# Ordering a few small TensorE products behind named dense products in a two-layer hybrid decoder trunk

## The chip, the core and the metric

The kernel runs on one core of one Trainium2 chip. The metric is the device time of one execution in microseconds (us), as the median of several runs. The core's engines are named as the profile names them: PE is TensorE, PEld its loads of weights, DVE is VectorE, ACT is ScalarE, POOL is GpSimd, and SP is the engine whose queue issues the DMA transfers.

## The reference, cut to what matters

Two layers are computed for 512 tokens of width 1024, in float32. Each layer norms its input, projects it, feeds three branches in parallel, merges them by gates, and ends with a wide MLP.

```python
xn = rmsnorm(x, norm1_g)
proj = xn @ w_in
y_ssd = ssd_mixer(...)      # chunked state-space scan, 2 groups of 8 heads, chunks of 128 tokens
y_mla = mla_mixer(...)      # latent attention, 8 heads
y_gdn = gdn_mixer(...)      # gated delta rule, 8 value heads, chunks of 64 tokens
mixed = g_ssd * (y_ssd @ w_ssd_out) + g_mla * (y_mla @ w_mla_out) + g_gdn * (y_gdn @ w_gdn_out)
h = x + mixed @ w_out
x = h + jnp.square(relu(rmsnorm(h, norm2_g) @ w_up)) @ w_down
```

Within a chunk the state-space branch multiplies its tokens by a decayed matrix of products of B and C (`y_diag`), adds what the state of the earlier chunks gives, multiplies by a gate and norms each group. The delta rule needs, for each chunk, the matrix of products of its keys, weighted by decays, and the inverse of that matrix plus the identity.

## The kernel before, in words

**Dense products.** Every large product is made by `dense_F` (or by its transposed twin). Operands are split into a high and a low part in a 32-bit format that PE takes in one pass, and `mm3` (lines 182 to 184) makes three PE instructions of each 128x128 by 128x512 product: high by high, high by low, low by high. A product with 256 output columns and 1024 inputs is 48 such instructions. Its weights come in four pairs of 128-row steps: each pair holds 12 instructions (column tile 0 with both steps, then column tile 1), and is split by a cast on ACT (L154) and a subtraction on DVE (L155). The split tiles rotate through four buffers, so that a cast waits until PE has finished with the pair four before. Raw weights come by DMA on SP's queue (L161).

**Small products.** Transpositions, chunk products and state updates are plain float32 instructions. They write to three rotating PSUM banks (`sm_bank`), with a fourth one apart (`y_bank`); dense products have four of their own.

**Order of the work.** The kernel is written in Tile: the text gives each instruction a place, and a scheduler of the compiler builds the queue of each engine from a model of the durations. An instruction earlier in the text goes first if its inputs are ready in that model; if not, later work is put ahead of it. `tc.high_priority()` lifts the splits (L154, L155) and the convolutions (L700 to L704). On the chip each engine takes its queue in order, and an instruction whose input is late holds what is queued behind it.

**The order around the change.** Per layer, the text reads: first state-space group, the decays of the delta rule (`gdn_decays`), the first half of the attention's output (`out_proj` with parts 0 and 1), second state-space group, the other half (parts 2 and 3), key products of the delta rule, and the state-space branch's output product. Each part of `out_proj` is a gate product (48 dense instructions on the normed input, `xh` and `xl` in the profile), then an output product (48 on the branch's result, `yh` and `yl`). So the scan of a state-space group, which has many small steps, is laid between the dense instructions of the gate and output product that follow it in the text.

- `ssd_group`, t = 0 to 3: products of B and C (L756), masked on DVE (L758), times the decays (L760), which ACT makes from a broadcast row (L467, L468, loaded at L465); then **the decay products** (L765, 8 products, 16 PE records), added on DVE (L767); for t > 0 the part of the earlier state (L774 to L776); the state update (L779, L781, L784 to L787); the gate (L790), squares (L792 to L794) and their sums (L795).
- After the four blocks: **the norm factors** (`rsq`: DVE L258, then a power on POOL, L259), **their transposition** on PE (L799), a copy on ACT (L801), a write to DRAM and a broadcast read (L802, L804 on SP), and the normed result (L808) with its split.
- `key_tiles` makes 256 key columns by a dense product, then convolution taps on ACT and DVE (L700, L704) and an activation that ends in DVE L263 and gives the tiles `ft`.
- `gdn_matrix(u, kT)`: **the key products** of four token tiles (L846), their masked copies and diagonal sums on DVE (L850, L851), then the power on POOL (L853, L855, L856) and the matrices (L861, L869). Unit 0 is called after the first `key_tiles`, so its products run among the dense instructions of the second `key_tiles`; unit 1 is called by `between` within the output product of the state-space branch. `gdn_blocks` and `gdn_inverse` use both units' matrices later (first PE step L925, fed by the copies at L919).

Of the kernel before, what the change touches and what calls it, by code (L numbers as in the profile page):

```python
# [20 lines left out]
P = 128  # L21
S = 512
T = S // P
D = 1024
# [31 lines left out]
def hybrid_kernel(ctx, tc, a, out, depth=2, taps=None):  # L56
# [89 lines left out]
        act.activation(cosT, nn, AF.Sin)  # L146


    def split_half(raw, hold=None, first=True):

        n = raw.shape[1]
        hi, lo = hold or (mk(wp, [P, n], F32R, "whi"), mk(wp, [P, n], F32R, "wlo"))
        with tc.high_priority() if first else nullcontext():
            act.copy(hi, raw)  # L154
            dve.tensor_tensor(lo, raw, f32(hi), ALU.subtract)  # L155
        return hi, lo
# [8 lines left out]
    def weights(w2d, c0, n, K, hold=None, raw0=None):  # L165

        kt = min(1024 // n, K // P)  # L170
        step = 512 // n
        for k0 in range(0, K // P, kt):
            given = raw0 is not None and k0 == 0
            raw = raw0 if given else weights_raw(w2d, c0, n, k0, kt)
            for q in range(0, kt, step):
                hi, lo = split_half(raw[:, q * n : (q + step) * n], hold and hold[k0 + q], not given)
                v = lambda x: x.rearrange("p (k n) -> p k n", n=n)
                yield k0 + q, v(hi), v(lo)

    def mm3(o, ah, al, bh, bl, start, stop, more=False):  # L180

        pe.matmul(o, ah, bh, start=start, stop=False, skip_group_check=more)  # L182
        pe.matmul(o, ah, bl, start=False, stop=False, skip_group_check=more)  # L183
        pe.matmul(o, al, bh, start=False, stop=stop, skip_group_check=more)  # L184

    def dense_F(gen, cols, K, xh, xl, mid=None, banks=None, after=None):

        pss = banks or [acc_bank() for _ in cols]
        last = K // P - 1
        if mid:
            gen = list(gen)
            for i, hf in enumerate(HALVES):
                for ps, c in zip(pss, cols):
                    for k0, wh, wl in gen:
                        for k in range(wh.shape[1]):  # L200
                            kk = k0 + k
                            mm3(ps[:, hf], wh[:, k, c], wl[:, k, c], xh[kk][:, hf], xl[kk][:, hf], kk == 0, kk == last)
                if i == 0:
                    mid()
            return pss
        for k0, wh, wl in gen:
            for ps, c in zip(pss, cols):
                for k in range(wh.shape[1]):
                    a_, b_ = wh[:, k, c], wl[:, k, c]
                    mm3(ps[: a_.shape[1], :], a_, b_, xh[k0 + k], xl[k0 + k], k0 + k == 0, k0 + k == last)  # L210
            if after:
                after()
        return pss
# [145 lines left out]
    xh, xl = hilo_tags(lp, "x")  # L359
# [4 lines left out]
    for ly in range(depth):  # L364
# [107 lines left out]
        def out_proj(w2d, br, yh, yl, pl, part=range(4), after=None, make=None, gate_banks=lambda: None):  # L472
            for dp in part:
                tg = []
                for j, ps in enumerate(dense_F(weights(w_in, O_GATE + br * D + dp * 256, 256, D), tiles(256), D, xh, xl, None, gate_banks(), after)):
                    t_ = make(dp, j) if make else mk(pl, [P, S], F32, "cva", 2)
                    act.activation(t_, ps, AF.Tanh, scale=0.5)
                    tg.append(t_)
                for j, ps in enumerate(dense_F(weights(w2d, dp * 256, 256, D), tiles(256), D, yh, yl, after=after)):
                    d = 2 * dp + j  # L480
                    if mixed[d] is None:
                        mixed[d] = mk(lp, [P, S], F32, "mix", 8)
                        dve.scalar_tensor_tensor(mixed[d], tg[j], 1.0, ps, ALU.add, ALU.mult)
                    else:
                        with tc.high_priority() if make else nullcontext():
                            dve.scalar_tensor_tensor(tg[j], tg[j], 1.0, ps, ALU.add, ALU.mult)
                            dve.tensor_tensor(mixed[d], mixed[d], tg[j], ALU.add)
# [227 lines left out]
        def ssd_group(g, yh, yl):  # L715
# [34 lines left out]
            for t in range(T):  # L750
                tok = slice(t * P, (t + 1) * P)
                e2 = [mk(br, [P, 4, P], F32, "eE", 4) for _ in range(2)]
                for q in range(2):
                    seg_exp(e2[q], t, h0 + 4 * q)
                ps = sm_bank()
                pe.matmul(ps[:, :P], bt[:, tok], ctl[:, tok], start=True, stop=True)  # L756
                cb = mk(br, [P, P], F32, "gk", 2)
                dve.scalar_tensor_tensor(cb, ps[:, :P], 0.25, incl, ALU.mult, ALU.mult)  # L758
                for e in e2:
                    dve.tensor_tensor(e, e, bc_mid(cb, 4), ALU.mult)  # L760
                py = sm_bank()
                for c in range(4):
                    for i in range(2):
                        h = 2 * c + i
                        pe.matmul(py[64 * i : 64 * i + 64, c * P : (c + 1) * P], xd[:, t, h * 64 : (h + 1) * 64], e2[h // 4][:, h % 4, :], start=True, stop=True)  # L765
                y = xf[:, :, tok]
                dve.tensor_tensor(y, y, c4(py), ALU.add)  # L767
                if t > 0:
                    eb = mk(br, [P, 4, P], F32, f"wk{t % 2}")
                    for i in range(2):  # L770
                        sync.dma_start(eb[64 * i : 64 * i + 64], d_p.rearrange("t (n l) -> t n l", l=P)[t, h0 + i : h0 + 8 : 2].partition_broadcast(64))
                    po = sm_bank()
                    for c in range(4):
                        pe.matmul(po[:, c * P : (c + 1) * P], st[:, c * P : (c + 1) * P], ctl[:, tok], start=True, stop=True)  # L774
                    dve.tensor_tensor(eb, c4(po), eb, ALU.mult)
                    dve.tensor_tensor(y, y, eb, ALU.add)  # L776
                if t < T - 1:
# [12 lines left out]
                dve.tensor_tensor(zt, zt, y, ALU.mult)  # L790
                sq = mk(br, [P, 4, P], F32, "wk2")
                act.activation(sq, zt, AF.Square)  # L792
                dve.tensor_tensor(sq[:, 0:2], sq[:, 0:2], sq[:, 2:4], ALU.add)
                dve.tensor_tensor(sq[:, 0], sq[:, 0], sq[:, 1], ALU.add)  # L794
                pe.matmul(pss[:, t : t + 1], sq[:, 0], ones[:, 0:1], start=True, stop=True)  # L795
            rs = mk(sp, [P, T], F32, "srs")
            rsq(rs, pss[:, :T], 1.0 / 512, EPS)
            ps = sm_bank()
            pe.transpose(ps[:T, :P], rs, ident)  # L799
            rsT = mk(br, [T, P], F32, "gk", 2)  # L800
            act.copy(rsT, ps[:T, :P])  # L801
            sync.dma_start(d_r[g].rearrange("(t p) -> t p", p=P), rsT)  # L802
# [19 lines left out]
        def key_tiles(c0, after=None):  # L822

            res = [mk(br, [P, S], F32, "ft", 6) for _ in range(2)]
            for i, ps in enumerate(dense_F(weights(w_in, O_GQ + c0 * P, 256, D), tiles(256), D, xh, xl, after=after)):
                gconv_silu(ps, c0 + i, res[i])
            return res

# [8 lines left out]
        def gdn_matrix(u, kT):  # L837
# [4 lines left out]
            for t in range(T):  # L842
                tok = slice(t * P, (t + 1) * P)
                pg = sm_bank()
                for i in range(2):
                    pe.matmul(pg[:, i * P : (i + 1) * P], kT[i][:, tok], kT[i][:, tok], start=True, stop=True)  # L846
                gk = mk(br, [P, 2, P], F32, f"wk{t}")
                for i in range(2):

                    dve.scalar_tensor_tensor(gk[:, i], hv(pg)[:, i], 1.0, ident, ALU.mult, ALU.mult, accum_out=ssq[:, i, t : t + 1])  # L850
                dve.tensor_tensor(gk, hv(pg)[:, 0:2], bc_mid(nstrict, 2), ALU.mult)  # L851
                gks.append(gk)
# [568 lines left out]
```

## Time and profile before

| | us |
|---|---|
| median of 3 runs | 2303.87 (2301.91 to 2304.52) |
| the profiled execution | 2301.75 |
| span of its first to last instruction | 2300.0 |
| PE busy | 2269.1 |
| DVE busy | 1645.3 |
| ACT busy | 1202.2 |
| POOL busy | 59.3 |

The profile is of one execution. A timeline row is: start in us from the span's start, duration, engine, line, operation, out<-in, shapes, count, and in brackets the idle time of the engine before it with what ended it. PE records overlap, since an instruction enters the array while the one before it is still in it: the distance from start to start tells what one costs, not the duration. In the view of waits a row is: who waited, for whom, us in total, times, longest. An idle time there counts from the modelled end of the instruction before. PE's granted clock was 0.999 of full speed over the span.

### The profile page before, as it was taken

To read this page: it belongs to the slowest core of one execution; us is meant where nothing else is said; L and a number is where in the kernel's file an instruction comes from. 1 tells how busy PE (TensorE), PEld (TensorE's weight loads), DVE (VectorE), ACT (ScalarE), POOL (GpSimd) and SP (SyncE) were. 2 spreads that over 40 slices of the span, in tenths; PEclk is the share of its full clock that TensorE was granted. 3 is DMA by queue.
4 is the path that set the end of the run, shared out by engine and by line. 5 is a ranking of instruction groups with operands and counts; after the bars stand their busy time and mean duration, and the time that the engine had idled before them with its cause. 6 is when DMAs were issued, how large, how long until landed. Compare 5 with 4: busy or idle time off the path is not lost.

```text
span 2300.0 us, 32300 instructions
## 1 busy us (share of the span) xinstructions
PE 2269.1 (99%) x11822; PEld 1864.8 (81%) x11822; DVE 1645.3 (72%) x3258; ACT 1202.2 (52%) x2508; POOL 59.3 (3%) x75
## 2 busy tenths in 40 slices
PE   9999999999999999999999999999999999999998
PEld 8788787888887888888888877878888877888886
DVE  7777566876667778767867775668657667778668
ACT  6766644334443465554657666443334435645545
POOL 0000000000000000000000000000000000000000
PEclk9999999999999999999999999999999999999999
DMA  4223634452224243233132236344422241433231
GB/s 144 81 74 101 193 101 119 126 141 75 87 69 165 65 147 108 86 109 111 53 99 78 79 108 195 95 113 141 126 77 83 65 165 56 160 106 101 92 110 46
DMA packets 220176, 244.23 MB, mean 106 GB/s; under 512 B 34272, under 2 KB 172528, under 8 KB 220016
## 3 DMA queue, kind: packets, MB, share of 16 engines
q1 hardware_dynamic: 220016, 242.16, 34.7%
q8 instruction: 93, 1.52, 0.3%
q14 instruction: 67, 0.55, 0.1%
HBM read 225.66 MB, written 11.74 MB: 103 GB/s over the span
## 4 chain that ended last, share of the span: by engine, by line
PE 89%; DVE 4%; ACT 2%; POOL 1%; issue 1%; DMA 0%; DVEq 0%; POOLq 0%; ACTq 0%; SPq 0%
PE acc L182 23%; PE acc L183 22%; PE acc L184 22%; PE sm L182 3%; PE sm L183 3%; PE sm L184 3%; DVE wlo L155 1%; PE sm L765 1%; PE sm L663 1%; ACT whi L154 1%; PE sm L1049 1%; POOL gms L259 1%; PE sm L774 1%; PE yt L679 1%; PE sm L643 1%
## 5 line engine op out<-in xcount | busy, mean ns | idle before, releaser
L155 DVE TENSOR_TENSOR wlo<-wraw,whi 128x512 fp32r<-128x512 f32 (+1 forms) x536 | 365.0, 685 | 344.8 <-ACT whi L154 338.2
L154 ACT CAST whi<-wraw 128x512 fp32r<-128x512 f32 (+1 forms) x536 | 329.7, 618 | 535.5 <-PE acc L183 365.3
L184 PE MATMUL acc<-xh,wlo 128*128 128x512 f32 (+1 forms) x1344 | 522.4, 389 | 0.0
L182 PE MATMUL acc<-xh,whi 128*128 128x512 f32 (+1 forms) x1344 | 522.2, 389 | 0.0
L183 PE MATMUL acc<-xl,whi 128*128 128x512 f32 (+1 forms) x1344 | 521.4, 388 | 0.0
L182 PEld LDWEIGHTS acc<-xh,whi 128*128 128x128 f32 x1344 | 252.7, 188 | 48.0 <-ACT xh L254 0.4
L183 PEld LDWEIGHTS acc<-xl,whi 128*128 128x128 f32 x1344 | 252.9, 188 | 47.7 <-DVE xl L255 0.7
L184 PEld LDWEIGHTS acc<-xh,wlo 128*128 128x128 f32 x1344 | 252.8, 188 | 47.7
L154 ACT CAST whi<-wr 128x512 fp32r<-128x512 f32 x168 | 104.3, 621 | 107.6 <-PE acc L183 47.5
L183 PE MATMUL acc<-yl,whi 128*128 128x512 f32 x384 | 151.4, 394 | 0.0
L182 PE MATMUL acc<-yh,whi 128*128 128x512 f32 x384 | 150.8, 396 | 0.0
L184 PE MATMUL acc<-yh,wlo 128*128 128x512 f32 x384 | 149.9, 390 | 0.0
L155 DVE TENSOR_TENSOR wlo<-wr,whi 128x512 fp32r<-128x512 f32 x168 | 113.2, 686 | 35.3 <-ACT whi L154 34.4
L704 DVE SCALAR_TENSOR_TENSOR ckl<-acc,pc,ckl 128x511 f32<-128x511 f32 (+2 forms) x168 | 120.3, 743 | 18.0 <-ACT ckl L700 10.8
L182 PEld LDWEIGHTS acc<-yh,whi 128*128 128x128 f32 x384 | 71.6, 188 | 16.0 <-ACT yh L254 1.7
L184 PEld LDWEIGHTS acc<-yh,wlo 128*128 128x128 f32 x384 | 72.2, 188 | 14.5
L183 PEld LDWEIGHTS acc<-yl,whi 128*128 128x128 f32 x384 | 72.2, 188 | 13.7
L183 PE MATMUL acc<-wlo,xh 128*128 128x512 f32 (+1 forms) x208 | 79.9, 384 | 0.0
L184 PE MATMUL acc<-whi,xl 128*128 128x512 f32 (+1 forms) x208 | 79.5, 384 | 0.0
L182 PE MATMUL acc<-whi,xh 128*128 128x512 f32 (+1 forms) x208 | 79.5, 384 | 0.0
L1161 DVE TENSOR_TENSOR h<-h,acc 128x512 f32<-128x512 f32 x120 | 76.9, 679 | 0.0
L467 ACT ACTIVATE eE<-eE,cum 128x128 f32<-128x128 f32 x192 | 63.2, 390 | 25.3 <-DMA eE<-d_c 22.2
(462 smaller groups left out, 4553.7 us busy)
## 6 DMA issues: line engine op xcount, KB each, us to landing
wraw<-in_w_in_dram SPq DMA_DIRECT2D x144, 512.0 KB, 3.6
wraw<-in_w_up_dram SPq DMA_DIRECT2D x64, 512.0 KB, 3.6
wr<-in_w_down_dram SPq DMA_DIRECT2D x32, 1024.0 KB, 5.3
eE<-d_c SPq DMA_DIRECT2D x48, 256.0 KB, 4.0
wraw<-in_w_mla_out_dram SPq DMA_DIRECT2D x16, 512.0 KB, 3.5
eE<-d_e SPq DMA_DIRECT2D x32, 256.0 KB, 2.8
wraw<-in_w_ssd_out_dram SPq DMA_DIRECT2D x16, 512.0 KB, 3.4
wraw<-in_w_gdn_out_dram SPq DMA_DIRECT2D x16, 512.0 KB, 3.4
```

What stands on the lines that cost most here:

```text
L154: act.copy(hi, raw)
L155: dve.tensor_tensor(lo, raw, f32(hi), ALU.subtract)
L182: pe.matmul(o, ah, bh, start=start, stop=False, skip_group_check=more)
L183: pe.matmul(o, ah, bl, start=False, stop=False, skip_group_check=more)
L184: pe.matmul(o, al, bh, start=False, stop=stop, skip_group_check=more)
L259: pool.tensor_tensor(o, o, (exp if exp is not None else nhalf)[:, : o.shape[1]], ALU.pow)
L467: act.activation(o[:, i], o[:, i], AF.Relu, scale=-1.0, bias=cum[:, t, h0 + i : h0 + i + 1])
L643: pe.matmul(o, qps[j][:, tok], kps[:, :n], start=False, stop=False)
L663: pe.transpose(ps[:, n : n + P], pn[t][:, kb * P : (kb + 1) * P], ident)
L679: pe.matmul(o, v_h, th[:, c : c + w], start=kb == 0, stop=False)
L704: dve.scalar_tensor_tensor(acc[:, d:], ps[:, : S - d], taps_[3 - d], acc[:, d:], ALU.mult, ALU.add)
L1161: dve.tensor_tensor(hs_, hs_, ps[t], op)
```

## The change

`behind(key, ins)` records that PE's instruction `ins` is to come after the dense product with that key; `place(key, ins)`, called by `dense_F` at the third instruction of each product, gives the key its instruction. The link (`NoSync`) is one for the scheduler's order alone: both instructions are PE's, and no semaphore is asked for. A key is (tag, row step k, column tile j). `dense_F` gets a tag from its callers: layer, branch, part and "g" (gate) or "y" (output) in `out_proj`, layer, "k" and the first key column tile in `key_tiles`.

```diff
+    def after_product(i, o):
+        tc.add_manual_dep(i, o.name, order_only, reason="behind a product")
+    def behind(key, ins):
+        if key in seen_at:
+            after_product(ins.ins, seen_at[key])
+        else:
+            awaiting.setdefault(key, []).append(ins.ins)
+    def place(key, ins):
+        seen_at[key] = ins.ins
+        for i in awaiting.pop(key, ()):
+            after_product(i, ins.ins)
...
-            for ps, c in zip(pss, cols):
+            for j, (ps, c) in enumerate(zip(pss, cols)):
                 for k in range(wh.shape[1]):
                     a_, b_ = wh[:, k, c], wl[:, k, c]
-                    mm3(ps[: a_.shape[1], :], a_, b_, xh[k0 + k], xl[k0 + k], k0 + k == 0, k0 + k == last)
+                    end = mm3(ps[: a_.shape[1], :], a_, b_, xh[k0 + k], xl[k0 + k], k0 + k == 0, k0 + k == last)
+                    place((tag, k0 + k, j), end)
...
-                        pe.matmul(py[64 * i : 64 * i + 64, c * P : (c + 1) * P], xd[:, t, h * 64 : (h + 1) * 64], e2[h // 4][:, h % 4, :], start=True, stop=True)
+                        x = pe.matmul(py[64 * i : 64 * i + 64, c * P : (c + 1) * P], xd[:, t, h * 64 : (h + 1) * 64], e2[h // 4][:, h % 4, :], start=True, stop=True)
+                        if t == 0:
+                            behind(((ly, 1, 2 * g, "g"), 2, 0), x)
...
-            pe.transpose(ps[:T, :P], rs, ident)
+            behind(((ly, 1, 2 * g, "y"), 6, 0), pe.transpose(ps[:T, :P], rs, ident))
...
-                    pe.matmul(pg[:, i * P : (i + 1) * P], kT[i][:, tok], kT[i][:, tok], start=True, stop=True)
+                    x = pe.matmul(pg[:, i * P : (i + 1) * P], kT[i][:, tok], kT[i][:, tok], start=True, stop=True)
+                    if u == 0:
+                        behind(((ly, "k", 6), *((4, 1) if t < 3 else (6, 0))), x)
```

So in each layer, for both state-space groups, the decay products of t = 0 come behind step 2, column tile 0 of the gate product of the part that follows the group, and the transposition of the norm factors behind step 6, column tile 0 of that part's output product. In each layer unit 0's key products come behind step 4, column tile 1 (tiles 0 to 2) and step 6, column tile 0 (tile 3) of the second key product. Nothing is computed otherwise.

More of the change, by code (lines that the diff above doesn't have):

```diff
@@ L146, in rope_tables @@
         act.activation(cosT, nn, AF.Sin)
+    seen_at, awaiting = {}, {}
+    order_only = mybir.DependencyInfo(mybir.DependencyClass.NoSync, mybir.DependencyReason.DATA)
+    def after_product(i, o):
[9 more added lines that the diff above has]
+            after_product(i, ins.ins)
     def split_half(raw, hold=None, first=True):
@@ L183, in mm3, with dense_F @@
         pe.matmul(o, ah, bl, start=False, stop=False, skip_group_check=more)
-        pe.matmul(o, al, bh, start=False, stop=stop, skip_group_check=more)
-    def dense_F(gen, cols, K, xh, xl, mid=None, banks=None, after=None):
+        return pe.matmul(o, al, bh, start=False, stop=stop, skip_group_check=more)
+    def dense_F(gen, cols, K, xh, xl, mid=None, banks=None, after=None, tag=None):
         pss = banks or [acc_bank() for _ in cols]
@@ L474, in out_proj @@
                 tg = []
-                for j, ps in enumerate(dense_F(weights(w_in, O_GATE + br * D + dp * 256, 256, D), tiles(256), D, xh, xl, None, gate_banks(), after)):
+                for j, ps in enumerate(dense_F(weights(w_in, O_GATE + br * D + dp * 256, 256, D), tiles(256), D, xh, xl, None, gate_banks(), after, (ly, br, dp, "g"))):
                     t_ = make(dp, j) if make else mk(pl, [P, S], F32, "cva", 2)
@@ L478, in out_proj @@
                     tg.append(t_)
-                for j, ps in enumerate(dense_F(weights(w2d, dp * 256, 256, D), tiles(256), D, yh, yl, after=after)):
+                for j, ps in enumerate(dense_F(weights(w2d, dp * 256, 256, D), tiles(256), D, yh, yl, after=after, tag=(ly, br, dp, "y"))):
                     d = 2 * dp + j
@@ L824, in key_tiles @@
             res = [mk(br, [P, S], F32, "ft", 6) for _ in range(2)]
-            for i, ps in enumerate(dense_F(weights(w_in, O_GQ + c0 * P, 256, D), tiles(256), D, xh, xl, after=after)):
+            for i, ps in enumerate(dense_F(weights(w_in, O_GQ + c0 * P, 256, D), tiles(256), D, xh, xl, after=after, tag=(ly, "k", c0))):
                 gconv_silu(ps, c0 + i, res[i])
```

## The prediction

> **What bounds the kernel now.** I read the page first (busy time, then the shares of the chain that ended last), next the view of waits for TensorE alone, and only then the timeline of the places that the change names.
>
> ```profile
> span 2300.0 us, 32300 instructions
> PE 2269.1 (99%) x11822; PEld 1864.8 (81%) x11822; DVE 1645.3 (72%) x3258; ACT 1202.2 (52%) x2508; POOL 59.3 (3%) x75
> ...
> PE 89%; DVE 4%; ACT 2%; POOL 1%; issue 1%; DMA 0%; DVEq 0%; POOLq 0%; ACTq 0%; SPq 0%
> ```
>
> The profiled execution took 2301.75 us: a span of 2300.0 and 1.75 around it. TensorE (PE) is busy for 99% of the span and holds 89% of the chain. So time goes only where PE's stream of products has a hole in it. The holes that these edits can reach are four rows of the waits; columns: total us, times, longest us.
>
> ```profile
> PE sm L799 <- POOL srs L259: 2.3, 4, 0.6
> PE sm L846 <- DVE ft L263: 1.7, 2, 0.8
> ...
> PE sm L765 <- ACT whi L154: 0.7, 3, 0.3
> PE sm L765 <- DVE eE L760: 0.5, 1, 0.5
> ```
>
> The reader is to see how small this is: 5.2 us in all. An idle time counts only from the modelled end of the product before it, so each hole is somewhat deeper. The timeline gives the measure (layer 0, first state-space group).
>
> ```profile
> 228.36 0.48 PE L182 MATMUL acc<-xh,whi 128*128 128x512 f32 x1
> ...
> 230.76 0.39 PE L183 MATMUL acc<-xl,whi 128*128 128x512 f32 x1
> 231.08 1.09 PE L765 MATMUL sm<-eE,tok 128*64 128x128 f32 x16
> ...
> 244.52 0.66 PE L765 MATMUL sm<-eE,tok 128*64 128x128 f32 x8 [0.20 <-ACT whi L154]
> ...
> 249.92 0.39 PE L182 MATMUL acc<-yh,whi 128*128 128x512 f32 x1
> ...
> 260.77 0.40 PE L184 MATMUL acc<-yh,wlo 128*128 128x512 f32 x1
> 261.70 0.27 PE L799 MATMUL sm<-ct,srs 128*4 128x128 f32 x1 [0.54 <-POOL srs L259]
> 261.73 0.48 PE L182 MATMUL acc<-yh,whi 128*128 128x512 f32 x1
> 262.04 0.39 PE L183 MATMUL acc<-yl,whi 128*128 128x512 f32 x1
> ...
> 265.24 0.39 PE L182 MATMUL acc<-xh,whi 128*128 128x512 f32 x1
> ...
> 268.64 0.39 PE L182 MATMUL acc<-xh,whi 128*128 128x512 f32 x1
> ```
>
> A dense product starts every 0.227 us when nothing is between ((268.64 - 265.24) / 15 starts), though its record lasts 0.39; a hole therefore costs 0.39 - 0.227 = 0.16 us more than the waits show. The one after a small product takes 0.31 (261.73 to 262.04): a switch costs 0.09. Entering L765 takes 0.32 (230.76 to 231.08), the same 0.09. One 256-wide dense product is 48 such instructions, so the gate product begins at 228.36: L765 stands behind its 11th instruction (rows 228.36 to 230.76 are 11), and the transposition L799 behind the 33rd instruction of the product that begins at 249.92 (249.92 to 260.77 are 33).
>
> **The change part by part.** It adds no instruction and, on paper, no semaphore: only the order in PE's queue changes. All keys are counted in dense instructions: ("g", 2, 0) is number 15 of a gate product, ("y", 6, 0) number 39 of an output product, (4, 1) and (6, 0) numbers 33 and 39 of the key product.
>
> *Transposition (4 times, L799).* It moves from behind 33 to behind 39: six dense products, 6 x 0.227 = 1.36 us later. Today the 15 dense products queued behind it stand still while the factor's power on POOL ends.
>
> ```profile
> 260.64 1.01 POOL L259 TENSOR_TENSOR srs<-srs,nhalf 128x4 f32<-128x4 f32 x1 [196.34 <-DVE srs L258]
> ```
>
> The power ends at 261.65 and PE goes on at 261.70. The hole is 260.77 to 261.70 less 0.227 = 0.70 us; over the four, 2.3 + 4 x 0.16 = 2.9 us. With six products in front and everything else as it was, PE would arrive at 260.77 + 7 x 0.227 = 262.36, after the power: gain 2.9, the upper bound. If the whole chain of the group shifts by the four products of the next edit (0.91 us), the power ends at 262.56 and 0.25 us of each hole stay: gain 4 x 0.45 = 1.8 to 1.9, the lower bound. I take 2.4, the middle. What is issued later with it:
>
> ```profile
> 262.29 0.32 SPq L802 DMA_DIRECT2D d_r<-gk  x1
> ...
> 268.16 0.43 SPq L161 DMA_DIRECT2D wraw<-in_w_mla_out_dram  x1
> ```
> ```profile
> L808 DVE SCALAR_TENSOR_TENSOR yl<-tok,pc,ft x14: 743/744/752, 394.6 to 1545.3; 128x512 f32<-128x512 f32 x14
> ```
>
> ACT's copy L801 and the 2 KB write L802 move by up to 1.36 us; behind L802 in SP's queue stand decay transfers and, 5.9 us later, a weight load. The factors are first used for normed tiles near 390 us, over 100 us later for this group, so nothing waits for the lateness itself. POOL's order is untouched. If SP's cover were gone, the price would be at most the 1.36 us.
>
> *First block's products (4 times, L765 of t = 0).* They move from behind 11 to behind 15: 0.91 us. The entry of 0.09 has no real hole in it today, so nothing is won at this place. What follows in the group (state product, next block) hangs on the same three small banks, so I expect the group to move as one body, 0.91 us. A gain can come only from how the body then meets the weight splits. The hole in front of 244.52 shows it:
>
> ```profile
> 240.43 0.70 ACT L467 ACTIVATE eE<-eE,cum 128x128 f32<-128x128 f32 x2 [1.35 <-DMA eE<-d_c]
> 241.03 0.61 ACT L154 CAST whi<-wraw 128x512 fp32r<-128x512 f32 x1
> 241.67 0.69 DVE L155 TENSOR_TENSOR wlo<-wraw,whi 128x512 fp32r<-128x512 f32 x1 [0.57 <-ACT whi L154]
> ```
>
> ACT waits for a decay tile, its cast comes late, and DVE's L155 stands in the middle of the group's chain: 0.57 idle + 0.69 = about 1.2 us, overlap taken off. That cast waits for the release of the second pair of weights (number 23); with four more products ahead of the block, the release comes before the next block's products and the split can fall into an earlier idle time. Bounds: all L765 holes, 0.7 + 0.5 + 4 x 0.16 = 1.8 less the four entries of about 0.09, so 1.5 us won; one more split in each group's chain, 4 x 1.2 = 4.8 lost. I take 0.5 won, near nothing, because the row to which it is nearest, the entry of 0.09, is no hole.
>
> *Key products (twice, L846 of unit 0).*
>
> ```profile
> 413.66 0.39 PE L182 MATMUL acc<-xh,whi 128*128 128x512 f32 x1
> ...
> 419.56 1.50 PE L846 MATMUL sm<-ft 128*128 128x128 f32 x12
> ...
> 422.04 0.60 PE L846 MATMUL sm<-ft 128*128 128x128 f32 x4
> ...
> 432.25 0.39 PE L184 MATMUL acc<-xh,wlo 128*128 128x512 f32 x1
> 433.48 0.94 PE L846 MATMUL sm<-ft 128*128 128x128 f32 x6 [0.84 <-DVE ft L263]
> ```
>
> From 413.66 there are 26 dense instructions to unit 0's first three tiles and 5 more to its last. They move to 33 and 39: 1.6 and 1.8 us later. Neither has a hole today; the whole 1.7 us of the waits' row is unit 1's, which the diff does not order. But the chain of waits leads from that hole back through unit 0:
>
> ```profile
> 425.11 1.65 POOL gork L855
> ...
> 426.79 0.17 DVE gork L856
> ...
> 427.41 0.66 DVE ckl L704
> ```
> ```profile
> 425.19 0.69 ACT L700 ACTIVATE ckl<-acc,pc 128x512 f32<-128x512 f32 x1 [0.97 <-PE acc L184]
> ```
>
> The convolution of unit 1's key could start on DVE at 425.19 + 0.69 = 425.88, but its first tap runs at 427.41: in DVE's queue it stands behind L856, which waits for POOL's power. With unit 0 some 1.6 us later the power would start near 426.7, after the taps are ready; a plan that fills DVE by readiness then puts the taps first, 1.5 us earlier, and POOL's power beside them. Unit 1's hole is 433.48 - 432.25 - 0.227 = 1.0 us, 1.7 + 2 x 0.16 = 2.0 for both layers; 1.5 covers it, and I take 1.9. Bounds: 2.2 won, with a saved switch of 0.09 in each layer; on the other side unit 0's lateness goes on to the block inverses.
>
> ```profile
> 501.31 0.62 ACT L919 COPY tok<-wk 32x512 f32<-32x512 f32 x1 [3.31 <-DMA wk<-d_x]
> ```
> ```profile
> 502.94 1.20 PE L925 MATMUL sm<-wk,tok 32*32 32x32 f32 x64
> ```
>
> The inverses' blocks are in at 501.31, 1.6 us before PE asks for them. PE, 1.0 us faster, would leave 0.6; if all of 1.8 us arrived there, PE would wait 1.2 us, 2.4 in both layers. DVE's recovered idle time (1.5) speaks against it.
>
> One rule speaks against this step. First the rows: POOL's power for four columns takes 1.01 at 260.64, but 1.52 when it starts just behind a DVE split with two inputs in SBUF; a split that starts inside a power is not held (0.69), nor is that power (1.64).
>
> ```profile
> 626.83 1.52 POOL L259 TENSOR_TENSOR gms<-gms,nhalf 128x4 f32<-128x4 f32 x1 [17.58 <-DVE gms L258]
> ```
> ```profile
> 626.79 0.69 DVE L155 TENSOR_TENSOR wlo<-wraw,whi 128x512 fp32r<-128x512 f32 x1
> ...
> 443.68 0.69 DVE L155 TENSOR_TENSOR wlo<-wraw,whi 128x512 fp32r<-128x512 f32 x1 [0.46 <-ACT whi L154]
> ```
> ```profile
> 443.06 1.64 POOL L855 TENSOR_TENSOR gork<-gss,phalf 128x8 f32<-128x8 f32 x1 [16.31 <-DVE gss L853]
> ```
>
> The Trainium skill says in "SBUF — State Buffer", section "Who interferes with whom", that a VectorE instruction with two SBUF inputs and a GpSimd instruction that reads SBUF exclude each other, and that the second fully blocks. The trace agrees where DVE came first (626.79), and not where POOL came first (443.68). By the rule both orders would cost.
>
> **The sum.** -2.4 - 0.5 - 1.9 = -4.8 us: the profiled execution would go from 2301.75 to 2296.95. It lies 2.12 below the median of the runs shown, 2303.87, which I lower by the same amount: **2299.1 us**. The bounds of the terms give -2.9 - 1.5 - 2.2 = -6.6 and -1.8 + 4.8 + 2.4 = +5.4.
>
> **The rivals.**
> 1. *The body does better.* The group meets its splits so well that all L765 holes close, the transposition never waits, and unit 1's products fuse: -6.6, 2297.3. For it: 244.52's hole stands behind one late cast. Against: it needs three gains at once.
> 2. *Only the transposition pays.* The group shifts by 0.91 us and keeps its holes, and L856 stays ahead of the taps, so unit 1's hole only moves: -1.9, 2302.0. For it: unit 1's hole is not ordered by the diff at all. This is also the case in which the edges say less than they seem to.
> 3. *A held power.* As 2, but the later power starts behind a split and takes 1.52 - 1.01 = 0.5 longer, L856 ahead of the taps: -1.9 + 2 x 0.5 = -0.9, 2303.0. The page named above is the one that gives it; 443.06 speaks against it.
> 4. *Slower: splits in the chain.* DVE takes L155 in order. If the shifted body puts two more such waits for a cast into each group's chain, PE waits 2 x 1.2 us in each of the four, at the L765 entries: +9.6 - 1.9 - 1.8 = +5.9, 2309.8. One more in each gives only +4.8 - 3.7 = +1.1, 2305.0, so it is slower by a measurable amount from two on. It decides whether the release after number 23 lands before or behind the DVE work for the next block. For it: one such wait stands there now. Against: four more dense products in front make the release earlier.
>
> **How the numbers follow.** A run can tell about 0.2% from no change: 4.6 us, below 2299.3 or above 2308.5. Forecast 42% (its own range 2297.5 to 2301.5 lies on both sides of that border: 24% faster, 18% same); rival 1 20%, faster; rival 2 15% and rival 3 5%, same; rival 4 18%, of which 15% slower and 3% (one split) same. Together faster 44%, same 41%, slower 15%. The range reaches from below rival 1 to behind the case of one split, 2295 to 2306.5, and leaves the two-split case and little else out.
>
> **What would show it.** Right: L799 behind 39 dense instructions of its product with no wait for srs in the waits, or 0.25 us; L765 of t = 0 behind 15, and the group's last products at most 0.9 us later against the dense ones; L704 ahead of L856 on DVE near 426 us and the row "L846 <- DVE ft L263" gone; no wait in front of L925. Wrong: the same total idle time of PE under new names, L155 waits at the L765 entries, or a stage far from the named ones whose order of instructions has changed; the last I cannot price, for a plan by readiness may shift anything behind an edit.

## The result, and the profile after

The changed kernel takes 2296.11 us (median of 8 executions, 2294.95 to 2300.71) beside 2303.07 of the kernel before (8 executions, 2301.67 to 2304.52): a ratio of 0.9973 with a 95% interval of 0.9965 to 0.9982. The medians differ by 7.0 us; the ratio, which weighs all executions, gives 6.2 us (4.1 to 8.1). The profiled execution took 2296.46, a span of 2294.7 and 1.8 around it. Lines of code have moved by 18 to 23: the cast is L172 and the split L173, the transposition L820, the decay products L784, the state products L795, the square sums L816, the key products L867, the power L278 or L878, the taps L723, the inverses L948.

The first two lines of the page after:

```profile
span 2294.7 us, 32300 instructions
PE 2266.6 (99%) x11822; PEld 1863.0 (81%) x11822; DVE 1647.0 (72%) x3258; ACT 1205.9 (53%) x2508; POOL 59.5 (3%) x75
```

The same instructions, and PE as full as before. Its waits after (total us, times, longest us):

```profile
PE yt L816 <- DVE wk L815: 1.3, 4, 0.6
...
PE sm L662 <- ACT qps L628: 0.7, 1, 0.7
```

All four rows of before are gone, L799, L846 and both of L765. Of the new rows one of 1.3 us stands at the square sums, inside the change, and one at L662, far from it. The timeline after, at the transposition of layer 0's first group and then of its second:

```profile
260.69 0.35 PE L816 MATMUL yt<-ct,wk 128*128 128x1 f32 x2
...
261.32 1.01 POOL L278 TENSOR_TENSOR srs<-srs,nhalf 128x4 f32<-128x4 f32 x1 [196.82 <-DVE srs L277]
...
261.92 0.39 PE L202 MATMUL acc<-yh,wlo 128*128 128x512 f32 x1
...
262.39 0.27 PE L820 MATMUL sm<-ct,srs 128*4 128x128 f32 x1
```
```profile
375.12 1.01 POOL L278 TENSOR_TENSOR srs<-srs,nhalf 128x4 f32<-128x4 f32 x1 [112.79 <-DVE srs L277]
...
376.43 0.39 PE L202 MATMUL acc<-yh,wlo 128*128 128x512 f32 x1
376.66 0.27 PE L820 MATMUL sm<-ct,srs 128*4 128x128 f32 x1
```

In the first group the power ends at 262.33 and PE takes up the factor at 262.39, 262.39 - 261.92 - 0.227 = 0.24 us late; in the second it ends at 376.13 and PE arrives 0.5 us later (376.43 + 0.227 = 376.66). At layer 0's keys:

```profile
423.72 0.75 DVE L723 SCALAR_TENSOR_TENSOR ckl<-acc,pc,ckl 128x511 f32<-128x511 f32 x1
...
424.79 0.69 DVE L173 TENSOR_TENSOR wlo<-wraw,whi 128x512 fp32r<-128x512 f32 x1 [0.24 <-ACT whi L172]
...
429.43 0.16 DVE L879 TENSOR_SCALAR gork<-gork 128x8 f32<-128x8 f32 x1
```
```profile
424.62 1.64 POOL L878 TENSOR_TENSOR gork<-gss,phalf 128x8 f32<-128x8 f32 x1 [48.50 <-DVE gss L876]
```
```profile
430.36 0.94 PE L867 MATMUL sm<-ft 128*128 128x128 f32 x6
431.82 0.83 PE L867 MATMUL sm<-ft 128*128 128x128 f32 x6
```

The first tap runs at 423.72, ahead of the scale L879, and no wait is noted at unit 1's products.

**Where the time came from.** I summed the starts of PE's records over each group, from the first dense instruction of the gate product to the end of the output product, 96 dense instructions, and over the two stretches of the keys, one in each layer: 144 dense instructions from the first of the second key product on. A dense start counts 0.227, a switch 0.088, what is left of a step from a dense instruction is a hole (the 0.09 of each entry is in it), and the steps of the other products are their time. The 384 dense starts of the four groups are 87.2 us in either kernel and have no column; the 0.5 and 0.8 us that are then missing are dense steps a little over 0.227. Sums of four groups, in us; "changes" is how often in a group a decay product (64 columns of weights, 128\*64) and another small product (128\*128) follow each other with no dense one between:

| kernel | changes in a group | small products | switches | holes at the transposition | other holes | four groups | both key stretches |
|---|---|---|---|---|---|---|---|
| before | 14 | 51.2 | 2.5 | 3.0 | 3.8 | 148.2 | 75.0 |
| changed | 10 | 47.8 | 3.5 | 0.5 | 3.6 | 143.4 | 73.0 |

That is 4.8 + 2.0 = 6.8 us; 1.5 us came back elsewhere in the profiled execution (2301.75 to 2296.46 is 5.3), 0.9 of it in one stretch that ends near 1265 us. There the new wait at L662 stands: a cast on ACT (L628) waits for a transfer, 0.56 us in the kernel before, 1.47 in the changed one and 2.65 in experiment 5, where the stretch took 3.6 more than before, a part of it at a lower clock (told at the end). PE's order at that place is the same in all kernels. The medians give 7.0.

### The profile page after: what moved, and what is told of

It is laid out like the page before. It is cut to its first block, busy times and chain, and to the rows that moved or that the text cites. A ratio compares the mean times of both kernels' runs of the same rounds, so it can differ in the third digit from the quotient of the medians.

```text
span 2294.7 us, 32300 instructions
## 1 busy us (share of the span) xinstructions
PE 2266.6 (99%) x11822; PEld 1863.0 (81%) x11822; DVE 1647.0 (72%) x3258; ACT 1205.9 (53%) x2508; POOL 59.5 (3%) x75
## 5 line engine op out<-in xcount | busy, mean ns | idle before, releaser
L172 ACT CAST whi<-wraw 128x512 fp32r<-128x512 f32 (+1 forms) x536 | 330.6, 620 | 531.9 <-PE acc L201 367.2
L173 DVE TENSOR_TENSOR wlo<-wraw,whi 128x512 fp32r<-128x512 f32 (+1 forms) x536 | 365.3, 686 | 339.5 <-ACT whi L172 334.0
L202 PEld LDWEIGHTS acc<-xh,wlo 128*128 128x128 f32 x1344 | 252.7, 188 | 47.8
L200 PEld LDWEIGHTS acc<-xh,whi 128*128 128x128 f32 x1344 | 252.6, 188 | 47.8 <-ACT xh L273 0.4
L172 ACT CAST whi<-wr 128x512 fp32r<-128x512 f32 x168 | 104.6, 623 | 107.4 <-PE acc L201 47.4
L173 DVE TENSOR_TENSOR wlo<-wr,whi 128x512 fp32r<-128x512 f32 x168 | 113.4, 688 | 35.4 <-ACT whi L172 34.7
L723 DVE SCALAR_TENSOR_TENSOR ckl<-acc,pc,ckl 128x511 f32<-128x511 f32 (+2 forms) x168 | 120.3, 744 | 18.0 <-ACT ckl L719 10.8
```

What stands on the lines that cost most here:

```text
L202: return pe.matmul(o, al, bh, start=False, stop=stop, skip_group_check=more)
L723: dve.scalar_tensor_tensor(acc[:, d:], ps[:, : S - d], taps_[3 - d], acc[:, d:], ALU.mult, ALU.add)
```

## The experiments

All are the changed kernel with the edit shown; medians of 11 executions against a before of 2302.55 to 2302.63 unless said otherwise. The three orders are called by their products: transposition, first block, keys; `t == 9` and `u == 9` never hold, which takes an order out.

**1. The transposition alone.**

```diff
-                        if t == 0:
+                        if t == 9:
...
-                    if u == 0:
+                    if u == 9:
```

> Only the transposition's order is kept, the other two are dropped. Theory (the six products in front cover the end of the POOL power, and nothing else moves with them): the four holes of 0.70 to 0.78 us go fully, since the power then ends about 0.7 us before TensorE gets there, 3.0 us in all, and the groups' small products stay as before, 12.8 us in each: 2303.07 - 3.0 = 2300.1. Rival (each later product moves the power's end along, so that the hole only changes its place): holes of the same 0.7 us, 2303.

2299.38, ratio 0.9987 (0.9978 to 0.9995). No hole is left at any of the four, and the small products took 51.2 as before; groups 144.9, 3.3 less. The power ends at 260.72 and the transposition runs at 261.47 after a dense product, with no wait:

```profile
259.71 1.01 POOL L278 TENSOR_TENSOR srs<-srs,nhalf 128x4 f32<-128x4 f32 x1 [196.00 <-DVE srs L277]
...
261.47 0.27 PE L820 MATMUL sm<-ct,srs 128*4 128x128 f32 x1
```

**2. The first block alone.**

```diff
-            behind(((ly, 1, 2 * g, "y"), 6, 0), pe.transpose(ps[:T, :P], rs, ident))
+            pe.transpose(ps[:T, :P], rs, ident)
...
-                    if u == 0:
+                    if u == 9:
```

> Only the first block's products are ordered. Theory (the group's body gains 2.4 us in all four, but its chain is 0.7 us later, and the transposition, left behind 33 products, waits for that): the transposition's holes grow from 0.7 and 0.8 to about 1.6 in the first group and 0.9 in the second group of each layer, 2.0 us lost, and the whole is -0.4: 2302.7. Rival (the parts add up, each by what its stage shows in the changed kernel): -2.4, 2300.7.

2301.12, ratio 0.9997 (0.9988 to 1.0005). The time by the clock does not tell the two apart. The groups do, against the theory: 145.8, 2.4 less than before, with small products of 47.7, switches of 3.5 and holes of 3.3 at the transposition. They hardly grew, since the plan itself put the transposition behind 36 dense instructions in each first group, not 33. The whole shows only 0.7 (by the ratio) to 1.5 us (by the medians) of that. A part of the difference goes with the granted clock: the profiled execution lost 2.8 us to stretches at half clock, told at the end, and four of the eleven executions have a mean clock of 0.997, as none of the 33 of before has. The six at 0.999 have a median of 2300.2 beside 2302.1 for the 18 of before at that clock, 1.9 less. The rest stays open.

**3. The keys alone.**

```diff
-                        if t == 0:
+                        if t == 9:
...
-            behind(((ly, 1, 2 * g, "y"), 6, 0), pe.transpose(ps[:T, :P], rs, ident))
+            pe.transpose(ps[:T, :P], rs, ident)
```

> Only unit 0's key products are ordered. Theory (the taps of unit 1's convolution pass ahead of the scale that waits for the POOL power): unit 1's hole goes from 1.00 to under 0.1 in each layer, the inverses do not wait, -2.0: 2301.1. Rival (the gain needs the groups ahead of it to be earlier, or it moves the hole to the inverses): the hole stays or the same microsecond turns up in front of the inverses, 0 to -0.2, 2303.

2299.96, ratio 0.9990 (0.9981 to 0.9999). Unit 1's hole is 0.09 in each layer instead of 1.00, both key stretches 73.0, and no wait stands at the inverses.

**4. No order on PE; on DVE, the scale behind its unit's last decay factor.** The three orders are out as in 1 to 3, and:

```diff
-            dve.tensor_scalar(ork, ork, 0.5, None, ALU.mult)
+            half = dve.tensor_scalar(ork, ork, 0.5, None, ALU.mult)
...
-            dve.tensor_tensor(cd, cc, dec[:, 1, :, hd0 : hd0 + 4], ALU.mult)
+            end = dve.tensor_tensor(cd, cc, dec[:, 1, :, hd0 : hd0 + 4], ALU.mult)
+            after_product(half.ins, end.ins)
```

> None of the three orders; instead the scale by one half that reads the POOL power is ordered on DVE behind the last decay factor of its unit, and the key products stay where they were before. Theory (DVE's queue standing behind that scale, and nothing about TensorE's order, makes unit 1's hole): the first tap starts near 426 us in the first layer instead of 427.4, unit 1's hole of 1.00 closes to under 0.2 in each layer, -1.6 to -2.0: 2301.2. Rival (the hole is the load of unit 0's other DVE work, or the place of its products in TensorE's queue): the hole stays above 0.6, at most -0.8, 2302.5.

2300.23, ratio 0.9990 (0.9981 to 0.9999). The first tap runs at 425.19, the scale (L879) not before 437.0, and the hole is gone in both layers; key stretches 72.7.

```profile
424.35 0.20 DVE L881 RECIPROCAL grk<-gss 128x8 f32<-128x8 f32 x1
425.19 0.75 DVE L723 SCALAR_TENSOR_TENSOR ckl<-acc,pc,ckl 128x511 f32<-128x511 f32 x1
```

So the hole was made by DVE's queue standing behind one small instruction that waits for POOL; moving PE's products is one way to get the taps past it, and not the only one.

**5. Transposition and keys, without the first block.**

```diff
-                        if t == 0:
+                        if t == 9:
```

> The transposition and the key products are ordered, the first block's products are not. Theory (three separate gains): -3.1 and -2.0 as in the runs with one order alone, -5.1 in all: 2297.8 beside a before of 2302.9; small products stay at 12.8 us in each group, holes at the transposition and at unit 1 are gone. Rival (the first block's order is what lets the transposition arrive late enough, or carries the rest): as much as the whole change, -7, 2296; or under -4, 2299.

2298.15, ratio 0.9978 (0.9969 to 0.9987), 5.1 us less at the ratio. Small products 51.2, 14 changes, no hole at the transposition, groups 145.0, keys 73.1. The two add up; what the first block brings to the whole is 145.04 - 143.37 = 1.7 here, and 2.1 without the 0.5 us at the transposition that come with it.

**6. As 5, with each square sum behind the next block's decay products.**

```diff
+                if t > 0:
+                    after_product(sums.ins, x.ins)
                 y = xf[:, :, tok]
...
-                pe.matmul(pss[:, t : t + 1], sq[:, 0], ones[:, 0:1], start=True, stop=True)
+                sums = pe.matmul(pss[:, t : t + 1], sq[:, 0], ones[:, 0:1], start=True, stop=True)
```

> As the run before (no order for the first block's products), but each block's square sum (L816 of t) is ordered behind the last decay product (L784) of block t + 1, so that no sum stands between decay products; nothing is moved against the dense products. Theory of the change of width (each extra run of 64-column decay products between 128-column ones costs about 0.44 us: 0.10 on its last, 0.16 on its first, 0.10 on the next product's first, 0.09 on the last one before; 9 runs a group become 7, as in the changed kernel): small products 12.8 to 11.9 us in each group, -3.5 against the run before: 2294.3. Rival (the first block's order wins by its place against the weight releases alone): small products 12.8, no change against the run before, 2297.8.

2293.36 (5 executions), ratio 0.9962 (0.9950 to 0.9975). Changes 10, small products 48.2, 3.0 less than in 5, switches still 2.5, groups 142.2: lower than the changed kernel's, and every small product stands behind the same dense instruction as in 5.

**7. Everything grouped.**

```diff
+            at = {0: ('g', 2, 0), 1: ('g', 4, 0), 2: ('g', 7, 1), 3: ('y', 3, 0)}
...
-                        if t == 0:
-                            behind(((ly, 1, 2 * g, "g"), 2, 0), x)
+                        if t in at:
+                            behind(((ly, 1, 2 * g, at[t][0]), *at[t][1:]), x)
+                if t > 0:
+                    after_product(sums.ins, x.ins)
...
-                        pe.matmul(po[:, c * P : (c + 1) * P], st[:, c * P : (c + 1) * P], ctl[:, tok], start=True, stop=True)
+                        after_product(pe.matmul(po[:, c * P : (c + 1) * P], st[:, c * P : (c + 1) * P], ctl[:, tok], start=True, stop=True).ins, x.ins)
...
-                pe.matmul(pss[:, t : t + 1], sq[:, 0], ones[:, 0:1], start=True, stop=True)
+                sums = pe.matmul(pss[:, t : t + 1], sq[:, 0], ones[:, 0:1], start=True, stop=True)
...
-            behind(((ly, 1, 2 * g, "y"), 6, 0), pe.transpose(ps[:T, :P], rs, ident))
+            behind(((ly, 1, 2 * g, "y"), 7, 1), pe.transpose(ps[:T, :P], rs, ident))
```

> The changed kernel with more order: the decay products (L784) of blocks 1, 2 and 3 stand behind instructions 27 and 48 of the gate product and 18 of the output product, each block's state products (L797) and the sum of the block before stand behind its last decay product, and the transposition stands behind the whole output product. Theory of the change of width: 4 runs of decay products in a group instead of 7, small products 11.9 to 10.6 us, 6 switches instead of 9 (-0.26), the holes of 0.24 at the transposition and of 0.3 to 0.8 at the sums gone (-0.4 a group): -7 to -8 against the changed kernel, 2288.5. Rival (the products kept together wait for DVE's second half, or the later chain holds the transposition): holes of 0.5 to 1 us in front of each L784, same as the changed kernel or slower, 2296 to 2300.

2291.81 (5 executions), ratio 0.9953 (0.9941 to 0.9966): faster than both kernels, 4.3 us under the changed one, not the 7 to 8 expected. Changes 4, small products 44.4, switches 2.1, no hole at the transposition; but other holes 4.1. Two of the miss's parts are in the rows: the small products cost 11.0 a group and not 10.6, and the last block's sum (L819 in this kernel) now waits, 1.6 us in the first groups of the two layers together:

```profile
259.33 0.35 PE L819 MATMUL yt<-ct,wk 128*128 128x1 f32 x2 [0.82 <-ACT eE L486]
```

**8. The first block behind 12 instead of 15.**

```diff
-                            behind(((ly, 1, 2 * g, "g"), 2, 0), x)
+                            behind(((ly, 1, 2 * g, "g"), 1, 1), x)
```

> The changed kernel with the first block's products behind instruction 12 of the gate product instead of 15. Theory (the next block comes 10 dense products behind, at 22, ahead of the release of the second weight pair behind 23, so that the split stays in the chain of block 2): its 16 decay products come in two halves with a wait of 0.1 to 0.4 us in front, small products 12.3 to 12.8, the total of the four groups 1.5 to 2.5 us longer than in the changed kernel. Rival (any shift of the first block does it): as the changed kernel, within 0.5 us.

2297.56 (one execution). The theory saw the place rightly: block 2's decay products come in two halves, 2.8 us apart, with holes of up to 0.4 us in front, since the split is in their chain again.

```profile
244.37 0.66 PE L784 MATMUL sm<-eE,tok 128*64 128x128 f32 x8
...
247.15 0.66 PE L784 MATMUL sm<-eE,tok 128*64 128x128 f32 x8
```

And it was wrong on the time: groups 143.4, the changed kernel's to the tenth, with 9 changes, small products of 48.6 and other holes of 3.1. The rival holds for this place, or nearly: without the holes at the transposition it is 143.4 beside 142.9 (one profile).

**9. As 7, with the last sum later.**

```diff
+            behind(((ly, 1, 2 * g, "y"), 6, 0), sums)
             rs = mk(sp, [P, T], F32, "srs")
```

> The grouped kernel, with the last block's square sum ordered behind 39 dense instructions of the output product instead of 34 or 35. Theory (that sum stood in front of TensorE's queue while ACT and DVE still made its square: holes of 0.98, 0.95 and twice 0.33): 4 or 5 dense products in front cover it, the transposition behind 48 still has 9 dense products of 0.227 us for the power, -2.2 to -2.6 against the grouped kernel: 2289.5. Rival (the sum's lateness goes on to the power and the transposition): the same time in front of the transposition, 2291.8.

2291.09 (5 executions), ratio 0.9950 (0.9937 to 0.9962), 0.7 under kernel 7 and not told apart from it. The groups fell by 1.5 to 137.0, other holes to 2.0; decay products waited for DVE within a run in its place (small products 45.0), and the rest went in stretches that the edit does not touch.

**10. As 7, with decay and state products made to alternate** (3 rounds, 10 executions).

```diff
+                xs = []
                 for c in range(4):
...
+                        xs.append(x)
...
-                        after_product(pe.matmul(po[:, c * P : (c + 1) * P], st[:, c * P : (c + 1) * P], ctl[:, tok], start=True, stop=True).ins, x.ins)
+                        w = pe.matmul(po[:, c * P : (c + 1) * P], st[:, c * P : (c + 1) * P], ctl[:, tok], start=True, stop=True)
+                        after_product(w.ins, xs[2 * c + 1].ins)
+                        for n in xs[2 * c + 2 : 2 * c + 4]:
+                            after_product(n.ins, w.ins)
```

> The grouped kernel with its decay products (64 columns) and state products (128 columns) of blocks 1 to 3 made to alternate, two and one, in the same places against the dense products: 13 runs of decay products a group instead of 4, the same instructions. Theory of the change of width: 0.30 to 0.45 us a run, 9 runs, 2.7 to 4.0 us a group, +11 to +16 in all, 2303 to 2308, with hardly a wait more in the records. Rival (the time of the small products is set by what they wait for, not by their neighbours): as the grouped kernel, 2291.8, within 1.

2302.40, ratio to before 1.0001 (0.9992 to 1.0011), 10.6 over kernel 7. Changes 22, small products 56.5, 12.1 more than in 7, with no wait at the decay or state products in the rows. This is the plainest proof. Block 1 of layer 0's first group in kernels 5, 6, 7 and 10: the same 16 records of decay products, 2 of a sum and 8 of state products (L795, L797, L798, L800), up to the start of the next (L802, L804, L805, L810). The decay products are L784, L785 or L786 here and the sum L816, L818, L819 or L824:

```profile
234.69 0.40 PE L784 MATMUL sm<-eE,tok 128*64 128x128 f32 x2
235.02 0.38 PE L816 MATMUL yt<-ct,wk 128*128 128x1 f32 x2
235.33 0.65 PE L784 MATMUL sm<-eE,tok 128*64 128x128 f32 x6
235.91 0.71 PE L795 MATMUL sm<-ckh,st 128*128 128x128 f32 x4
236.55 0.66 PE L784 MATMUL sm<-eE,tok 128*64 128x128 f32 x8
237.14 0.71 PE L795 MATMUL sm<-ckh,st 128*128 128x128 f32 x4
237.69 1.02 PE L802 MATMUL sm<-wk,kt 128*128 128x512 f32 x2
```
```profile
234.81 0.66 PE L784 MATMUL sm<-eE,tok 128*64 128x128 f32 x8
235.39 0.71 PE L797 MATMUL sm<-ckh,st 128*128 128x128 f32 x4
236.03 0.66 PE L784 MATMUL sm<-eE,tok 128*64 128x128 f32 x8
236.62 0.38 PE L818 MATMUL yt<-ct,wk 128*128 128x1 f32 x2
236.87 0.69 PE L797 MATMUL sm<-ckh,st 128*128 128x128 f32 x4
237.39 1.02 PE L804 MATMUL sm<-wk,kt 128*128 128x512 f32 x2
```
```profile
236.47 1.09 PE L785 MATMUL sm<-eE,tok 128*64 128x128 f32 x16
237.49 0.38 PE L819 MATMUL yt<-ct,wk 128*128 128x1 f32 x2
237.74 1.14 PE L798 MATMUL sm<-ckh,st 128*128 128x128 f32 x8
238.71 1.02 PE L805 MATMUL sm<-wk,kt 128*128 128x512 f32 x2
```
```profile
237.16 0.44 PE L786 MATMUL sm<-eE,tok 128*64 128x128 f32 x4
237.52 0.49 PE L800 MATMUL sm<-ckh,st 128*128 128x128 f32 x2
237.94 0.44 PE L786 MATMUL sm<-eE,tok 128*64 128x128 f32 x4
...
240.44 1.02 PE L810 MATMUL sm<-wk,kt 128*128 128x512 f32 x2
```

3.00 us with 5 changes, 2.58 with 3, 2.24 with one, 3.28 with 7: some 0.17 us a change ((3.28 - 2.24) / 6), and no bracket of a wait in any row. Over the four groups it is the same: 12.1 us for 18 changes more in each, 0.17 apiece. A run of four decay records takes 0.36 with a dense product in front and a product of 128 columns behind, where 16 take 1.02.

**11. The first block behind 24.**

```diff
-                            behind(((ly, 1, 2 * g, "g"), 2, 0), x)
+                            behind(((ly, 1, 2 * g, "g"), 3, 1), x)
```

> The changed kernel with the first block's products behind instruction 24 of the gate product instead of 15: behind the release of the second weight pair, which is behind 23. Theory as predicted (a split that falls ahead of the block leaves the chain): the total of the four groups as in the changed kernel or better, 143.4 us or less. Rival (only the runs of decay products count, 8 a group here as behind 12, and the holes that the later chain makes): small products 12.1 as behind 12, total 143.4 plus the wait at the transposition, which comes 9 dense products later in the chain: up to 1 us a group more.

2300.72 (one execution). The rival again: 9 changes, small products 48.6, but holes of 3.0 at the transposition and 4.9 elsewhere, groups 148.2. Without the holes at the transposition that is 145.1, which lies within what kernels 1, 3, 4 and 5 take, which leave the first block alone (144.5 to 145.4): a later place does not win by itself. The later chain pays at its end:

```profile
257.70 0.35 PE L816 MATMUL yt<-ct,wk 128*128 128x1 f32 x2 [0.91 <-DVE wk L815]
...
263.32 0.27 PE L820 MATMUL sm<-ct,srs 128*4 128x128 f32 x1 [0.54 <-POOL srs L278]
```

## Why the prediction was right, and where it was not

*Transposition, -2.4: right.* The four holes lost 2.5 us. The price that was named for a chain shifted by 0.91 us, 0.25 left of each hole, is what the first groups show (0.24); the second groups' chains came earlier and left none. So two holes fell near the lower bound and two near the upper, and the middle, 2.4, came out by that mixture, which the prediction did not foresee. Alone it is the upper bound: all 3.0 us of holes, predicted 2.9.

*Keys, -1.9: right, in size and in mechanism.* 2.0 us, with the first tap ahead of the scale; experiment 4 takes the wait away on DVE and leaves PE's order alone, and the hole goes just the same. The lateness did not reach the inverses. The blocks come in at 497.21 and PE asks at 499.75, a slack of 2.5 us where 0.6 was feared, since they came 4.1 earlier and PE 3.2 (that DVE's regained idle time is the reason, as the prediction argued, no experiment tests):

```profile
497.21 0.62 ACT L942 COPY tok<-wk 32x512 f32<-32x512 f32 x1 [2.40 <-DMA wk<-d_x]
...
499.75 1.20 PE L948 MATMUL sm<-wk,tok 32*32 32x32 f32 x64
```

*A held power: did not come.* The power at 424.62 took its 1.64 though a split started 0.17 us into it (424.79, 0.69). All four powers of the keys took 1.64, and all four of the factors 1.01. The rule cited for that rival, of the Trainium skill's "SBUF — State Buffer", section "Who interferes with whom", is once more not what the trace shows where POOL came first.

*First block, -0.5: the mis-sized term.* The mechanism that was named did happen. In layer 0 the second split falls into the idle time of block 1, and block 2's products come in one piece, with both halves ready:

```profile
237.60 0.69 DVE L173 TENSOR_TENSOR wlo<-wraw,whi 128x512 fp32r<-128x512 f32 x1 [0.35 <-ACT whi L172]
...
244.13 1.09 PE L784 MATMUL sm<-eE,tok 128*64 128x128 f32 x16
...
252.56 0.35 PE L816 MATMUL yt<-ct,wk 128*128 128x1 f32 x2 [0.33 <-DVE wk L815]
```

But as a matter of waits it was worth next to nothing: holes of 0.36, 0.38, 0.10 and 0.41 in front of block 2 fell to the entry's 0.09, and so did one of 0.70 in front of block 3; in their place sums that now stand alone among dense products wait for DVE (0.49, 0.76 and twice 0.34, the first of them at 252.56). Other holes went from 3.8 to 3.6 only. What the block's order won lies in products that never waited: the small products took 51.24 - 47.76 = 3.5 less, because the plan made 10 changes of shape in a group and not 14: two fewer at block 2, whose products come in one piece, and two fewer at block 3, whose products the sum no longer interrupts. 1.0 went back for three more switches a group. By the groups' totals without the transposition's holes that is 145.26 - 142.89 = 2.4, and 1.6 to 2.5 against the five kernels (before, 1, 3, 4 and 5) whose groups otherwise have the order of before, since their other holes spread from 3.1 to 4.0. The step that failed is "Bounds: all L765 holes ... so 1.5 us won": it took the small products' own time as fixed, and so counted holes alone. Experiments 6 against 5 and 10 against 7 show that it is not fixed, in both directions and with the small products' places among the dense ones kept (but for the last sum of a group in 10, which came four or five dense instructions later); 8 suggests, in one profile, that the release in front of the next block is not needed for the gain, and 11 that holes elsewhere can eat it up. The Trainium skill has a rule that fits, in "TensorEngine Tiling (Array Packing)", section "Tiling Modes", under "Key Properties": a change of tiling mode, and not just of the tile, drains the engine. The trace agrees in so far as a change between products with 64 and 128 columns of weights costs about 0.17 us; that a drain is what costs it, no record shows.

*The sum, -4.8: too small by 2.2 at the medians, nearly all of it this term* (-2.5 - 2.0 - 2.4 by the stages). The price is rival 1's, -6.6, but its mechanism only in part: the holes in front of the decay products did close, but sums opened others, the transposition still waits in the first groups, and unit 1's products still come in two pieces (430.36 and 431.82). The slower rival did not come either: no hole in front of the decay products is over 0.1 us. That a block placed later can cost what it wins, experiment 11 shows.

## What to carry to other kernels

On an engine that is 99% busy, holes are not all that order changes: products of one shape kept together cost less than the same products interleaved with another shape, and the records show it only in the distance from start to start. Ordering a consumer behind named work pays when it just covers its producer's end; placed further back, it can be paid for at the end of the chain (experiment 11). And where a queue stands behind one small instruction that waits for a slow engine, move that instruction: it is worth as much as moving the whole stage.

## What the runs showed of the hardware beside

Apart from the first and last microseconds, TensorE's granted clock fell to half for some 3.4 us in four of the thirteen profiles. In experiments 2 and 3 (twice each) and 10 (once) it did so behind the wait of 0.9 to 1.2 us at L524 (L505 before) that every kernel has; in experiment 5 once, from 1246.1 on, behind the wait of 1.9 us at L662. The windows of experiment 2 (us from the start: length, PE busy and its records, granted clock, DMA share, GB/s), and its timeline:

```profile
1200.00:1204.00 4.00, 2.96 (x19) 0.90 0.26 90
1204.00:1208.00 4.00, 4.00 (x13) 0.67 0.03 9
1208.00:1212.00 4.00, 4.00 (x32) 1.00 0.36 89
```
```profile
1201.05 1.23 PE L524 MATMUL sm<-ct,yh 128*128 128x128 f32 x8 [1.16 <-DVE yh L519]
...
1203.24 0.63 PE L202 MATMUL acc<-cqh,wlo 128*128 128x512 f32 x1
1203.67 0.63 PE L200 MATMUL acc<-cqh,whi 128*128 128x512 f32 x1
```

Dense products start every 0.43 us there instead of 0.227, PE counts as fully busy, and a stretch in experiments 2, 3 and 10 costs 1.2 to 1.6 us with no wait in the records. The order at these places is the same in all kernels; why it happens in some executions stays open. It is a part of the spread of single executions here, about 4 us: in experiment 2 the four executions with a mean clock of 0.997 have a median of 2303.5, the six at 0.999 one of 2300.2. That is a reason to compare stages rather than spans.
